# Output projection by token block: whole w_out on chip, merged activations through DRAM

## The chip, the core and the metric

The kernel runs on one NeuronCore of a Trainium2 chip. The metric is device time in microseconds (us) of one execution; lower is better. A profile is one execution recorded by the hardware profiler. The engines are TensorE (PE in the profile, with its weight loads as PEld), VectorE (DVE), ScalarE (ACT), GpSimd (POOL) and SyncE (SP), which here only issues DMA transfers. A "q" behind an engine's name is that engine's instruction queue.

## The reference

One decoder layer over 1,040 tokens (16 meta tokens and 1,024 real ones) with 1,024 channels, in float32:

```python
h = concat(meta, x)
xn = rms_norm(h, g_pre_mix)
# short gated convolution and stick-breaking attention, both on xn
merged = gate_conv * (y_conv @ w_proj_conv) + gate_attn * (o @ w_proj_attn)
mix = merged @ w_out                       # the output projection: the change is here
h = h + rms_norm(mix, g_post_mix)
ffn = conv_gated_mlp(rms_norm(h, g_pre_ffn), w_up_gate, conv_w_ffn, w_down)
h = h + rms_norm(ffn, g_post_ffn)
return h[:, 16:, :]
```

## The kernel before

Only the last 1,026 tokens are needed behind the attention (14 of the meta tokens drop out). They stand as 3 chunks of 342 (CH) or 9 blocks of 114 tokens (QB). Every float32 product is made of three matmuls in fp32r: each operand is split into a rounded part and the rest (`split`, lines 63 to 65: the rounded part by an ACT copy, the rest by a DVE or POOL subtraction), and hi x hi, hi x lo and lo x hi are added up in PSUM. The contraction over 1,024 channels takes 8 steps, so one output tile is 24 matmuls.

The stages around the change, in the order of the program:

- Branch projections, run by `Dense` (lines 80 to 153). An item is one block of 128 output channels, with all 1,026 tokens moving in 3 chunks, 72 matmuls of 342 columns in all. Its weights are loaded two items ahead and split one item ahead (ACT, and POOL for the rest). `item_pc` (8 items) multiplies the convolution branch by its gate and stores it to `m_d` in DRAM. `item_pa` (lines 598 to 613, 8 items) loads the attention gate and that stored product, multiplies by the gate on DVE straight from PSUM (L610), adds on POOL (L611), and splits the merged activations into `mT` (L612), which stands for all tokens on chip in the three slots A, B and C. These slots held `yT`, the convolution output, until the last `item_pc`.
- Output projection (lines 667 to 762). A tile `out_block` has the 114 tokens of a block as its stationary operand and 256 columns of w_out moving (L673 to L675). w_out is split a quarter at a time (`load_wq`, two quarters on chip). The loop takes blocks 0 to 5 through all four quarters, then blocks 6 to 8 through all four, so w_out is loaded and split twice. An evacuation is an ACT Square that sums squares along the row (L679) and a DVE multiplication by g_post into a row buffer of a ring of six (L680).
- Behind the fourth quarter of a block comes `post_block` (lines 682 to 707): the norm's factor from the sum of squares (`rstd_of`, L72 to L77, five small DVE instructions and one ACT square root), h = row x factor + x on DVE in place (L694), the store of h to `h_d` (L695), an ACT Square over h into the x buffer (L697), a second factor, and the normalised row on DVE (L699), which is written over h in the same row buffer. Later `transposed` turns this row by 8 PE transposes (L174) and splits the result (ACT and DVE, L64 and L65 with tile xn) into `xn2`, the FFN's input.
- FFN: `Dense` again, over `xn2`. Its first four chunks are interleaved by hand with the last transposes (lines 765 to 770).

PSUM has 3 buffers for the output projection's tiles, 2 for transposes, 3 for `Dense`. The framework's scheduler fixes the order of instructions on every engine when the kernel is built: among those whose operands it reckons to be ready it takes the first in the order of the program, so a load or a group of matmuls can stand ahead of where the program names it. On the chip each engine then runs its queue strictly in order, and semaphores hold an instruction until its operands are there.

## Time and profile before

| | us |
|---|---|
| median of 3 runs | 2127.32 |
| lowest and highest run | 2126.53, 2127.89 |
| time of the profiled execution | 2128.91 |
| its span, first to last instruction | 2126.8 |

The profiled execution stands 1.6 us above the median; 2.1 us of it lie outside the span. In views of the profile, a gap in square brackets behind a row is how long its engine had been idle ahead of it and what ended that; "granted clock" (PEclk) is the share of TensorE's full clock of 2.4 GHz, 0.50 being its lower level of 1.2 GHz.

### The profile page before, as it was taken

The numbers are of one execution on the slowest core, as the hardware profiler recorded it, in microseconds if no ns is written. First come the engines' busy times: TensorE is split into PE (matmuls) and PEld (weight loads), VectorE is DVE, ScalarE is ACT, GpSimd is POOL, SyncE is SP. The second block draws the span as 40 slices with busy tenths as digits, with TensorE's granted clock in tenths as the row PEclk, the third lists the DMA queues.
The fourth block names the chain that finished last, engine by engine and source line by source line (L and its number), as shares of the span: only waits on it lengthen the run. The fifth ranks groups of instructions, "written<-read, shape, count | busy, mean of one in ns | idle before, by whom it ended". The sixth has DMA issues, their size and how long they took to land.

```text
span 2126.8 us, 31235 instructions
## 1 busy us (share of the span) xinstructions
PE 2048.7 (96%) x12840; PEld 1965.7 (92%) x12840; DVE 1028.5 (48%) x1623; ACT 798.1 (38%) x1667; POOL 706.4 (33%) x597
## 2 busy tenths in 40 slices
PE   5999999999999999999999998899999999999997
PEld 5999999999999999999999998899999999999996
DVE  6455565556555555654231424544333334343436
ACT  4444454545554545544421224432222222222232
POOL 4343444344343534443122432222122221222123
PEclk9999999999999999999999999899999999999999
DMA  3111101111111111111674433411111111111023
GB/s 131 41 50 44 57 31 60 41 50 41 47 44 51 50 41 51 40 60 60 199 228 134 135 126 109 149 63 41 40 54 56 50 40 40 50 60 50 31 80 139
DMA packets 42538, 152.17 MB, mean 72 GB/s; under 512 B 4744, under 2 KB 4744, under 8 KB 42396
## 3 DMA queue, kind: packets, MB, share of 16 engines
q1 hardware_dynamic: 41244, 148.09, 21.2%
q8 instruction: 100, 1.64, 0.3%
q10 hardware_dynamic: 1152, 2.10, 0.3%
q14 instruction: 42, 0.34, 0.1%
HBM read 120.76 MB, written 29.41 MB: 71 GB/s over the span
## 4 chain that ended last, share of the span: by engine, by line
PE 86%; DVE 7%; ACT 3%; DMA 2%; issue 1%; POOL 0%; DVEq 0%; ACTq 0%; SPq 0%; POOLq 0%
PE mm L124 21%; PE mm L125 21%; PE mm L126 20%; PE po L808 3%; PE po L807 3%; PE tp L368 3%; PE po L809 3%; PE av L358 2%; PE av L359 2%; PE z L322 2%; PE z L321 2%; DMA h_d<-owork 1%; DVE fl L332 1%; DVE yy L193 1%; PE po L674 1%
## 5 line engine op out<-in xcount | busy, mean ns | idle before, releaser
L124 PE MATMUL mm<-xnT,whi 128*128 128x342 f32 (+2 forms) x1536 | 508.0, 331 | 3.6 <-ACT xnT L64 3.6
L65 POOL TENSOR_TENSOR wlo<-raw,whi 128x1024 fp32r<-128x1024 f32 x124 | 312.6, 2521 | 576.0 <-ACT whi L64 576.0
L125 PE MATMUL mm<-xnT,whi 128*128 128x342 f32 (+2 forms) x1536 | 495.1, 322 | 0.5 <-DVE xnT L65 0.5
L126 PE MATMUL mm<-xnT,wlo 128*128 128x342 f32 (+2 forms) x1536 | 493.5, 321 | 0.0
L124 PE MATMUL mm<-xn,whi 128*128 128x342 f32 (+1 forms) x1056 | 338.1, 320 | 0.0
L125 PE MATMUL mm<-xn,whi 128*128 128x342 f32 (+1 forms) x1056 | 337.1, 319 | 0.0
L126 PE MATMUL mm<-xn,wlo 128*128 128x342 f32 (+1 forms) x1056 | 336.5, 319 | 0.0
L334 POOL TENSOR_TENSOR be<-be,fl 114x127 f32<-114x127 f32 (+2 forms) x144 | 176.8, 1227 | 404.0 <-DVE fl L332 195.1
L124 PEld LDWEIGHTS mm<-xnT,whi 128*128 128x128 f32 x1536 | 291.1, 190 | 8.4 <-ACT xnT L64 4.2
L125 PEld LDWEIGHTS mm<-xnT,whi 128*128 128x128 f32 x1536 | 291.7, 190 | 2.1 <-DVE xnT L65 1.0
L126 PEld LDWEIGHTS mm<-xnT,wlo 128*128 128x128 f32 x1536 | 290.9, 189 | 0.0
L64 ACT CAST whi<-raw 128x1024 fp32r<-128x1024 f32 x126 | 132.3, 1050 | 265.8 <-PE mm L125 239.8
L332 DVE TENSOR_TENSOR_SCAN fl<-fl 114x128 f32<-114x128 f32 (+2 forms) x144 | 204.9, 1423 | 4.9
L125 PEld LDWEIGHTS mm<-xn,whi 128*128 128x128 f32 x1056 | 199.9, 189 | 2.7
L124 PEld LDWEIGHTS mm<-xn,whi 128*128 128x128 f32 x1056 | 199.2, 189 | 2.8
L126 PEld LDWEIGHTS mm<-xn,wlo 128*128 128x128 f32 x1056 | 199.3, 189 | 0.0
L65 DVE TENSOR_TENSOR al<-tp,ah 128x342 fp32r<-128x342 f32 (+4 forms) x288 | 127.0, 450 | 139.7 <-ACT ah L64 137.3
L814 DVE TENSOR_TENSOR acc<-acc,po 128x512 f32<-128x512 f32 x136 | 93.0, 685 | 189.1 <-PE po L809 189.1
L64 ACT CAST ah<-tp 128x342 fp32r<-128x342 f32 (+4 forms) x288 | 113.1, 398 | 189.7 <-PE tp L368 181.9
L323 ACT ACTIVATE fl<-z 114x348 f32<-114x348 f32 (+10 forms) x240 | 111.5, 465 | 130.7 <-PE z L322 123.4
L368 PE MATMUL tp<-ident,be 114*128 114x114 f32 x720 | 119.5, 263 | 25.6 <-DVE al L65 21.0
L368 PEld LDWEIGHTS tp<-ident,be 114*128 114x128 f32 x720 | 89.1, 138 | 40.2 <-DVE al L65 29.9
(160 smaller groups left out, 3569.6 us busy)
## 6 DMA issues: line engine op xcount, KB each, us to landing
raw<-in_w_in_dram SPq DMA_DIRECT2D x64, 512.0 KB
raw<-in_w_up_gate_dram SPq DMA_DIRECT2D x44, 512.0 KB
raw<-in_w_down_dram SPq DMA_DIRECT2D x22, 512.0 KB
raw<-in_w_out_dram SPq DMA_DIRECT2D x16, 512.0 KB
y_d<-yy SPq DMA_DIRECT2D x8, 513.0 KB
ga_d<-gt SPq DMA_DIRECT2D x8, 513.0 KB
o_d<-ot SPq DMA_DIRECT2D x8, 513.0 KB
gc_d<-gt SPq DMA_DIRECT2D x8, 513.0 KB
```

The lines of the kernel that those rows point to most:

```text
L64: nc.scalar.copy(hi, src)
L65: (lo_engine or nc.vector).tensor_tensor(lo, src, hi.bitcast(F32), op=ALU.subtract)
L124: nc.tensor.matmul(ps, wh, xh, start=(kb == 0), stop=False)
L125: nc.tensor.matmul(ps, wh, xl, start=False, stop=False)
L126: nc.tensor.matmul(ps, wl, xh, start=False, stop=(kb == KB - 1))
L323: nc.scalar.activation(fl[:, c0:c0 + n], z, AF.Sigmoid, scale=-0.125)
L332: nc.vector.tensor_tensor_scan(fl[:, :nk][:, ::-1], fl[:, :nk][:, ::-1], fl[:, :nk][:, ::-1], 1.0, op0=ALU.mult, op1=ALU.min)
L334: nc.gpsimd.tensor_tensor(be[:, 0:nk - 1], be[:, 0:nk - 1], fl[:, 1:nk], op=ALU.mult)
L368: nc.tensor.transpose(tp[:n, QB * j:QB * (j + 1)], blocks[j][0][:, kb * P:kb * P + n], ident[:QB, :QB])
L807: nc.tensor.matmul(ps, th, hi[:, c], start=(j == 0), stop=False)
L808: nc.tensor.matmul(ps, tl, hi[:, c], start=False, stop=False)
L814: nc.vector.tensor_tensor(a, a, ps, op=ALU.add)
```

## The change

`item_pa` no longer builds `mT`. Of its merged activations, blocks 0 and 1 are split at once into two tiles `mb`; the other seven blocks are stored, one DMA for each item, into a new DRAM tensor `mm_d` laid out by token block. w_out is loaded and split once, one block of 128 output columns with each `item_pa`, into slots A, B and C (`w_o`). The output projection then goes block by block, three tiles of 342, 342 and 340 columns each; block b + 1 is loaded from `mm_d` and split (ACT and DVE) while block b is multiplied. The ring of six rows becomes two row buffers, the normalised row is written into the x buffer instead of over h, and transposes follow one block behind. `xn2` has all its slots from the start. The FFN's two first convolution inputs move from the former ring to slot C.

```diff
     m_d = tc.dram_tile([D, NQ], F32, name="m_d")
+    mm_d = tc.dram_tile([7, P, KB * QB], F32, name="mm_d")
...
 
 
     at_ctx.close()
-    slots_r = ctx.enter_context(ExitStack())
-    slotA = ctx.enter_context(pool("slotA", 1, "right"))
-    slots_bc = ctx.enter_context(ExitStack())
-    slotB = slots_bc.enter_context(pool("slotB", 1, "right"))
-    slotC = slots_bc.enter_context(pool("slotC", 1, "right"))
+    slots_abc = ctx.enter_context(ExitStack())
+    slotA = slots_abc.enter_context(pool("slotA", 1, "right"))
+    slotB = slots_abc.enter_context(pool("slotB", 1, "right"))
+    slotC = slots_abc.enter_context(pool("slotC", 1, "right"))
     s_ctx = ctx.enter_context(ExitStack())
     sw = s_ctx.enter_context(pool("sw", 2, "right"))
     gp["p"], gp["n"] = sw, 2
...
     slots_de = ctx.enter_context(ExitStack())
     slotD = slots_de.enter_context(pool("slotD"))
     slotE = slots_de.enter_context(pool("slotE"))
-    slots_f = ctx.enter_context(ExitStack())
-    slotF = slots_f.enter_context(pool("slotF"))
-    wq_ctx = ctx.enter_context(ExitStack())
+    slotF = slots_de.enter_context(pool("slotF"))
+    m_ctx = ctx.enter_context(ExitStack())
+    mpool = m_ctx.enter_context(pool("mblk", 2))
     oT = [slot_tile(pl, "oT") for pl in (slotD, slotE, slotF)]
 
     CH3 = [(0, CH), (CH, CH), (2 * CH, CH)]
...
                 nc.sync.dma_start(m_d[ob * P:(ob + 1) * P, :], g[:, :NQ])
         return (col_block(w_proj_conv, ob), src_of(yT), CH3, evac)
 
-    mT = []
+    mb = {}
+
+    def m_tile(b):
+        mb[b] = mpool.tile([P, 2, KB, QB], F32R, name="mb", tag="mb")
+        return mb[b]
 
     def item_pa(ob):
         st = {}
 
         def evac(ci, a, n, ps):
             if ci == 0:
-                if ob == 0:
-                    mT.extend(slot_tile(pl, "mT") for pl in (slotA, slotB, slotC))
                 st["g"] = sw.tile([P, NT], F32, name="gal", tag="wk")
                 st["m"] = sw.tile([P, NT], F32, name="ml", tag="ld")
                 nc.sync.dma_start(st["g"][:, :NQ], ga_d[ob * P:(ob + 1) * P, :])
...
             g, m = st["g"][:, a:a + n], st["m"][:, a:a + n]
             nc.vector.tensor_tensor(g, g, ps, op=ALU.mult)
             nc.gpsimd.tensor_tensor(g, g, m, op=ALU.add)
-            split(mT[ci][:, 0, ob, :], mT[ci][:, 1, ob, :], g)
+            if ci == 0:
+                for b in range(2):
+                    t = mb.get(b)
+                    if t is None:
+                        t = m_tile(b)
+                    split(t[:, 0, ob, :], t[:, 1, ob, :], g[:, b * QB:(b + 1) * QB])
+            if ci == 2:
+                gv = st["g"][:, 2 * QB:NQ].rearrange("p (b n) -> p b n", n=QB)
+                nc.sync.dma_start(mm_d[:, :, ob * QB:(ob + 1) * QB].rearrange("b p n -> p b n"), gv)
         return (col_block(w_proj_attn, ob), src_of(oT), CH3, evac)
 
     items += [item_pc(ob) for ob in range(8)] + [item_pa(ob) for ob in range(8)]
...
         if k < 8:
             load_split(oT, o_d, k)
             k += 1
-    wq = wq_ctx.enter_context(pool("wq", 2))
-
-    def load_wq(qt):
-        hi = wq.tile([P, KB, 256], F32R, name="wqh", tag="wqh")
-        lo = wq.tile([P, KB, 256], F32R, name="wql", tag="wql")
-        for hf in range(2):
-            raw = wpool.tile([P, D], F32, name="raw", tag="raw")
-            rv = raw.rearrange("p (k n) -> p k n", k=KB)
-            nc.sync.dma_start(raw, w_out[2 * qt + hf])
-            split(hi[:, :, hf * P:(hf + 1) * P], lo[:, :, hf * P:(hf + 1) * P], rv, nc.gpsimd)
-        return hi, lo
-
-    wqs = []
+    w_o = [slot_tile(pl, "w_o") for pl in (slotA, slotB, slotC)]
+    wo_raw = {}
+
+    def load_wo(i):
+        wo_raw[i] = wpool.tile([P, D], F32, name="raw", tag="raw")
+        nc.sync.dma_start(wo_raw[i], w_out[i])
+
+    def split_wo(i):
+        rv = wo_raw.pop(i).rearrange("p (k n) -> p k n", k=KB)
+        for c in range(3):
+            a, e = max(i * P, c * CH), min((i + 1) * P, (c + 1) * CH, D)
+            if a < e:
+                o = slice(a - c * CH, e - c * CH)
+                split(w_o[c][:, 0, :, o], w_o[c][:, 1, :, o], rv[:, :, a - i * P:e - i * P], nc.gpsimd)
+
     for i in range(24):
+        if i % 3 == 0:
+            load_wo(i // 3)
         dense.chunk()
-        if i == 21:
-            wqs.append(load_wq(0))
+        if i % 3 == 1:
+            split_wo(i // 3)
     s_ctx.close()
     psA.close()
 
...
     nc.sync.dma_start(g_post, g_post_mix.partition_broadcast(P))
     nc.sync.dma_start(g_pre2, g_pre_ffn.partition_broadcast(P))
 
-    xn2 = [slot_tile(slotD, "xn2"), slot_tile(slotE, "xn2")]
-    wk = slotF.tile([P, 2, KB, CH], F32, name="owork", tag="t").rearrange("p a k n -> p (a k n)")
-    ring = [wk[:, i * D:(i + 1) * D] for i in range(5)]
-    ring.append(ow.tile([P, D], F32, name="ring5"))
+    xn2 = [slot_tile(pl, "xn2") for pl in (slotD, slotE, slotF)]
 
     ff_items, act, conv_in = [], {}, {}
     dense3 = Dense(ps_mm2, ff_items)
 
-    def out_block(b, qt, hi, lo, ssq):
-        ps = ps_o.tile([P, 512], F32, name="po", tag="po")[:QB, :256]
-        c, o = b // 3, (b % 3) * QB
+    rows = {}
+
+    def load_m(b):
+        if b in mb or b > 8:
+            return
+        raw = mpool.tile([P, KB, QB], F32, name="mraw", tag="mraw")
+        nc.sync.dma_start(raw, mm_d[b - 2].rearrange("p (k n) -> p k n", k=KB))
+        t = m_tile(b)
+        split(t[:, 0], t[:, 1], raw)
+
+    def out_chunk(b, c, ssq):
+        n = min(CH, D - c * CH)
+        ps = ps_o.tile([P, 512], F32, name="po", tag="po")[:QB, :n]
+        m = mb[b]
         for kb in range(KB):
-            mh = mT[c][:, 0, kb, o:o + QB]
-            ml = mT[c][:, 1, kb, o:o + QB]
-            nc.tensor.matmul(ps, mh, hi[:, kb, :], start=(kb == 0), stop=False)
-            nc.tensor.matmul(ps, ml, hi[:, kb, :], start=False, stop=False)
-            nc.tensor.matmul(ps, mh, lo[:, kb, :], start=False, stop=(kb == KB - 1))
-        cs = slice(qt * 256, (qt + 1) * 256)
-        dst = ring[b % 6][:QB, cs]
-        sq = ow.tile([P, 256], F32, name="sq", tag="sq")
-        nc.scalar.activation(sq[:QB], ps, AF.Square, accum_out=ssq[:QB, qt:qt + 1])
-        nc.vector.tensor_tensor(dst, ps, g_post[:QB, cs], op=ALU.mult)
+            mh, ml = m[:, 0, kb, :], m[:, 1, kb, :]
+            wh, wl = w_o[c][:, 0, kb, :n], w_o[c][:, 1, kb, :n]
+            nc.tensor.matmul(ps, mh, wh, start=(kb == 0), stop=False)
+            nc.tensor.matmul(ps, ml, wh, start=False, stop=False)
+            nc.tensor.matmul(ps, mh, wl, start=False, stop=(kb == KB - 1))
+        cs = slice(c * CH, c * CH + n)
+        sq = ow.tile([P, CH], F32, name="sq", tag="sq")
+        nc.scalar.activation(sq[:QB, :n], ps, AF.Square, accum_out=ssq[:QB, c:c + 1])
+        nc.vector.tensor_tensor(rows[b][:QB, cs], ps, g_post[:QB, cs], op=ALU.mult)
 
     def post_block(b, ssq):
         t = b * QB
-        h = ring[b % 6][:QB]
+        h = rows[b][:QB]
         xv = ow.tile([P, D], F32, name="xv", tag="xv", bufs=2)[:QB]
         if b == 0:
             nc.sync.dma_start(xv[0:2], meta_tokens[T0:NMETA, :])
...
         s2 = osml.tile([P, 1], F32, name="s2", tag="s2")
         nc.scalar.activation(xv, h, AF.Square, accum_out=s2[:QB])
         r2 = rstd_of(osml, s2, QB)
-        nc.vector.scalar_tensor_tensor(h, h, r2, g_pre2[:QB], op0=ALU.mult, op1=ALU.mult)
+        nc.vector.scalar_tensor_tensor(xv, h, r2, g_pre2[:QB], op0=ALU.mult, op1=ALU.mult)
 
         def transposed():
             c, o = b // 3, (b % 3) * QB
-            if b == 6:
-                xn2.append(slot_tile(slotA, "xn2"))
-            to_features(xn2[c][:, 0, :, o:o + QB], xn2[c][:, 1, :, o:o + QB], h, QB, ps_tp2)
+            to_features(xn2[c][:, 0, :, o:o + QB], xn2[c][:, 1, :, o:o + QB], xv, QB, ps_tp2)
 
         to_transpose.append(transposed)
 
...
     def item_u(fb):
         def evac(ci, a, n, ps):
             if ci == 0:
-                conv_in[fb] = (wk[:, 3072 + fb * NQ:3072 + (fb + 1) * NQ] if fb < 2 else
+                if fb == 0:
+                    wk = slotC.tile([P, 2, KB, CH], F32, name="owork", tag="t")
+                    ffn["wk"] = wk.rearrange("p a k n -> p (a k n)")
+                conv_in[fb] = (ffn["wk"][:, fb * NQ:(fb + 1) * NQ] if fb < 2 else
                                ffn["u"].tile([P, NQ], F32, name="u", tag="u"))
             u = conv_in[fb]
             nc.scalar.copy(u[:, a:a + n], ps)
...
         ff_items += [item_u(2 * gi), item_u(2 * gi + 1), item_g(2 * gi), item_g(2 * gi + 1)]
 
     to_transpose = []
-    DEFER = 3
-    sums = {}
-    for qi in range(8):
-        qt = qi % 4
-        hi, lo = wqs.pop(0)
-        if qi < 7:
-            wqs.append(load_wq((qi + 1) % 4))
-        blocks = range(6) if qi < 4 else range(6, 9)
-        for b in blocks:
-            if qt == 0:
-                sums[b] = osml.tile([P, 4], F32, name="sums", tag="sums", bufs=9)
-            out_block(b, qt, hi, lo, sums[b])
-            if qi == 6 and b == 6:
-                dense3.load(0)
-            if qi == 7 and b == 6:
-                dense3.prep(0)
-                dense3.load(1)
-            if to_transpose and len(to_transpose) >= (DEFER if qt == 3 else 1):
-                to_transpose.pop(0)()
-            if qt == 3:
-                post_block(b, sums[b])
+    for b in range(9):
+        load_m(b + 1)
+        rows[b] = ow.tile([P, D], F32, name="row", tag="row", bufs=2)
+        sums = osml.tile([P, 3], F32, name="sums", tag="sums")
+        for c in range(3):
+            out_chunk(b, c, sums)
+        if to_transpose:
+            to_transpose.pop(0)()
+        if b == 7:
+            dense3.load(0)
+            dense3.prep(0)
+            dense3.load(1)
+        post_block(b, sums)
 
 
     first = [dense3.run(0), dense3.run(1)]
...
         if to_transpose:
             to_transpose.pop(0)()
     o_ctx.close()
-    wq_ctx.close()
-    slots_f.close()
-    slots_bc.close()
+    slots_abc.close()
+    m_ctx.close()
     fu = ctx.enter_context(pool("fu", 2, "right"))
     fp = ctx.enter_context(pool("ffn", 2))
     fsml = ctx.enter_context(pool("fsml", 4))
```

## Rows read from the trace of the kernel before

**Rows 1.** The page's first part: span, and busy time, share of the span and instructions of each engine.

```profile
span 2126.8 us, 31235 instructions
PE 2048.7 (96%) x12840; PEld 1965.7 (92%) x12840; DVE 1028.5 (48%) x1623; ACT 798.1 (38%) x1667; POOL 706.4 (33%) x597
```

**Rows 2.** Busy time by stretch of the span: start and end in us, length, then busy time (and instructions) of each engine, granted clock, busy share of the 16 DMA engines, and GB/s. The stretches are four items of `item_pa`, the output projection up to the last transposes, and the FFN behind it.

```profile
1165.00:1210.40 45.40, 45.40 (x292) 45.40 (x291) 18.68 (x24) 9.97 (x17) 20.82 (x18) 1.00 0.42 140
...
1242.50:1387.90 145.40, 129.41 (x1010) 127.49 (x1009) 67.11 (x173) 54.03 (x145) 36.47 (x16) 0.94 0.34 114
1388.00:2080.00 692.00, 692.00 (x4003) 655.12 (x4002) 271.51 (x331) 173.46 (x247) 152.03 (x64) 1.00 0.16 52
```

**Rows 3.** TensorE's own instructions in order of time, the first ones of five groups of transposes: start, length, what, and the gap ahead of it. The fifth group stands behind the first chunk of the FFN.

```profile
1311.01 0.84 PE L174 MATMUL tp<-ident,owork 114*128 114x114 f32 x5 [4.12 <-DVE owork L699]
...
1317.01 0.39 PE L174 MATMUL tp<-ident,owork 114*128 114x114 f32 x2 [0.49 <-DVE owork L699]
...
1328.21 0.29 PE L174 MATMUL tp<-ident,owork 114*128 114x114 f32 x1 [4.44 <-DVE owork L699]
...
1343.27 0.43 PE L174 MATMUL tp<-ident,owork 114*128 114x114 f32 x1 [3.67 <-DVE owork L699]
...
1376.02 1.50 PE L174 MATMUL tp<-ident,owork 114*128 114x114 f32 x8 [2.95 <-DVE owork L699]
```

**Rows 4.** Busy time by stretch again (columns as in rows 2), for the four stretches within the output projection in which the granted clock was at its lower level.

```profile
1311.45:1314.86 3.41, 3.41 (x19) 3.41 (x18) 2.07 (x11) 1.78 (x6) 0.00 (x0) 0.50 0.39 156
1328.52:1331.93 3.41, 3.41 (x19) 3.41 (x18) 3.13 (x12) 1.82 (x6) 0.00 (x0) 0.50 0.59 231
1342.17:1348.99 6.82, 5.72 (x28) 5.75 (x29) 4.63 (x10) 2.69 (x7) 0.00 (x0) 0.50 0.56 172
1376.30:1379.71 3.41, 3.41 (x17) 3.41 (x15) 2.52 (x11) 2.37 (x6) 0.00 (x0) 0.50 0.34 139
```

**Rows 5.** The chain of work that ended last, from 1297 to 1388 us: its shares by line, and two of its longest pieces (start, length, what). Below it, from the waits of 1297 to 1388 us: engine, waiting line, what it waited for, us in total, times, longest.

```profile
by line: DMA h_d<-owork 29.0%; DVE owork L694 7.1%; DMA h_d<-ring 6.9%; DVE owork L699 5.7%; PE po L674 5.6%; PE po L675 5.5%; PE po L673 5.5%; PE tp L174 4.8%; issue 4.4%; DVE t L75 4.2%; DVE s L77 2.8%; ACT xv L697 2.2%; ACT sq L679 1.7%;
...
1305.77 9.72 DMA h_d<-owork
1371.22 9.25 DMA h_d<-owork
...
PE tp L174 <- DVE owork L699: 15.7, 5, 4.4
...
DVE owork L699 <- DMA h_d<-owork: 13.9, 7, 3.9
```

**Rows 6.** Two instructions that recur at TensorE's pace: an evacuation's Square (ACT) at the beginning and the end of nine tiles of 256 columns; a load of the stored product (SP's queue) of one item and of the item four later. Then a group of transposes and the matmul behind it (PE).

```profile
1265.45 0.39 ACT L679 ACTIVATE sq<-po 114x256 f32<-114x256 f32 x1 [2.35 <-PE po L675]
...
1290.94 0.38 ACT L679 ACTIVATE sq<-po 114x256 f32<-114x256 f32 x1 [2.36 <-PE po L675]
...
1165.24 0.32 SPq L608 DMA_DIRECT2D ml<-m_d  x1
...
1210.39 0.32 SPq L608 DMA_DIRECT2D ml<-m_d  x1
...
1387.20 0.94 PE L174 MATMUL tp<-ident,owork 114*128 114x114 f32 x8
1387.92 0.40 PE L124 MATMUL mm<-xn,whi 128*128 128x342 f32 x1
```

**Rows 7.** From the end of block 6's last tile to its normalised row, as ACT, DVE and SP's queue ran it (two blocks share some of the small instructions, hence x2).

```profile
1363.72 0.39 ACT L679 ACTIVATE sq<-po 114x256 f32<-114x256 f32 x1 [1.01 <-PE po L675]
...
1366.01 1.29 DVE L694 SCALAR_TENSOR_TENSOR owork<-owork,s,xv 114x1024 f32<-114x1024 f32 x1
...
1367.33 1.06 ACT L697 ACTIVATE xv<-owork 114x1024 f32<-114x1024 f32 x1 [0.29 <-DVE owork L694]
...
1367.33 0.29 SPq L695 DMA_DIRECT2D h_d<-owork  x1
...
1369.60 0.28 DVE L77 TENSOR_TENSOR s<-s,t 114x1 f32<-114x1 f32 x2
...
1374.58 1.29 DVE L699 SCALAR_TENSOR_TENSOR owork<-owork,s,g_pre 114x1024 f32<-114x1024 f32 x1 [3.39 <-DMA h_d<-owork]
```

**Rows 8.** Groups of instructions by line and shape: engine, operation, shape, count | busy us, mean ns of one | idle time ahead of them. The first four are of 1152 to 1242 us (`item_pa`), the last one of 1242 to 1388 us.

```profile
L611 POOL TENSOR_TENSOR gal<-gal,ml 128x342 f32<-128x342 f32 x22 | 20.4, 925 | 38.5 <-DVE gal L610 33.2 <-POOL wlo L65 3.7 <-issue 1.6
L65 POOL TENSOR_TENSOR wlo<-raw,whi 128x1024 fp32r<-128x1024 f32 x7 | 16.9, 2408 | 8.9 <-ACT whi L64 8.9
...
L610 DVE TENSOR_TENSOR gal<-gal,mm 128x342 f32<-128x342 f32 x22 | 11.1, 506 | 14.0 <-PE mm L126 14.0
...
L64 ACT CAST whi<-raw 128x1024 fp32r<-128x1024 f32 x7 | 7.4, 1053 | 18.9 <-PE mm L125 18.4 <-ACT mT L64 0.6
...
L65 DVE TENSOR_TENSOR xn<-tp,xn 128x456 fp32r<-128x456 f32 x16 | 9.8, 628 | 1.4 <-ACT xn L64 1.2
```

**Rows 9.** The DMA queue that all these transfers use (page: packets, MB, share of the time of the 16 DMA engines); and, in `item_pa`, a POOL addition and the load of the attention gate in SP's queue.

```profile
q1 hardware_dynamic: 41244, 148.09, 21.2%
...
1198.15 0.93 POOL L611 TENSOR_TENSOR gal<-gal,ml 128x342 f32<-128x342 f32 x1 [2.85 <-DVE gal L610]
...
1201.89 0.39 SPq L607 DMA_DIRECT2D gal<-ga_d  x1
```

## The prediction

> **What bounds the kernel now.** I began with the busy times of the whole span: TensorE is busy for 2048.7 of 2126.8 us [rows 1], so a change gains only what it takes off TensorE or off TensorE's idle time. The table by stretch says where that lies. In the branch projections TensorE is busy for all of 45.40 us at full clock, and in the FFN for all of 692.00 us; in the output projection it is busy for 129.41 of 145.40 us at a mean clock of 0.94 [rows 2]. So the stretch 1242.5 to 1387.9 us is the one to price.
>
> The gaps on TensorE there stand ahead of transposes: 4.12, 0.49, 4.44, 3.67 and 2.95 us, 15.67 us together, and each was ended by L699, the DVE instruction that makes the normalised row [rows 3]. With each of the four gaps of 2.95 us and more goes a stretch at the lower clock, which begins between 1.1 us ahead of the gap's end and 0.5 us behind it; the gap of 0.49 has none. These stretches last 17.05 us, 15.95 of them busy [rows 4], and half of the busy time, 8.0 us, is what the clock cost.
>
> What L699 waited for: it is written over h, which a DMA is still reading to store it. In the chain of waits that store holds 29.0% of the stretch 1297 to 1388 us, with pieces of 9.72 and 9.25 us, and 13.9 us of DVE's waits are L699 waiting for it [rows 5]. In block 6 everything but that wait took from 1363.72 (Square of the last tile) to 1369.88 (end of L77) and 1.29 for L699, 7.5 us; with the wait L699 ended at 1375.87, 12.2 us [rows 7]. Six blocks reach this tail one tile (2.8 us) apart, so all of it falls due at once.
>
> **The change part by part.**
>
> *The matmuls.* Nine tiles of 24 matmuls with 256 columns took 25.49 us, 2.832 us a tile; four items of three chunks with 342 columns took 45.15 us, 3.762 us a chunk [rows 6]. Before: 36 x 2.832 = 102.0 us. After: 27 x 3.762 = 101.6 us, less 0.2 for the last chunk's 340 columns. Wider tiles therefore gain 0.6 us at most, and I count 0.4. (The 342-column row has 128 stationary columns, the new tiles 114; the 256-column row has 114. I take no gain for that.) The transposes stay, 9 x 0.72 us [rows 6] = 6.5.
>
> *What stalls now cost.* The old stretch holds 102.0 + 6.5 + three FFN chunks of 3.76 = 119.8 us of work in 145.4 us. Lost: 25.6 us, of which the rows above name 15.7 of gaps and 8.0 of clock; the other 1.9 is restarts and smaller gaps.
>
> *The store's wait goes.* The normalised row is written to the x buffer, which nothing stores. Next late: the bare chain of 7.5 us. Per block it has now until the end of the following block, one group of transposes and three chunks: 0.72 + 11.29 = 12.0 us. Other DVE work can get in between: two evacuations of the next block at 0.51, two subtractions of transposes at 0.63 [rows 8], and the subtraction of `load_m` over 912 columns, about 1.2 us by L694's 1.29 for 1024 [rows 7]; together 3.5, so 11.0 of 12.0 us at worst. DVE's whole load of a block is some 8.3 us (three evacuations 1.5, L694 and L699 2.6, subtractions 2.5, small ones 1.7). TensorE waits for nothing here, with 1 us to spare at worst.
>
> *The last block.* Behind block 8 TensorE has only the transposes of block 7 (0.72) and FFN chunks. If the order holds block 8's transposes behind one chunk (3.76), as it held block 6's in the kernel before, they come 4.5 us after the tile, and the chain takes 7.7 (Square and evacuation are wider) to 9.0 us (with block 7's subtractions): a gap of 3.2 to 4.5 us, and 1.7 us of clock. If the order puts a second chunk ahead, 8.2 us are covered and the gap is 0 to 0.8. Bounds 0 and 6.2 us. Before, the wait was in the scheduler's reckoning as well; with a shorter chain it may still go for one chunk. I take 3.0.
>
> *w_out.* Eight loads and splits, not sixteen. In the old projection they ran on POOL and ACT off TensorE's path. Now one goes with each `item_pa`: POOL has 3 x 0.93 + 2.41 + one more 2.41 = 7.6 of 11.29 us [rows 8], ACT 1.05 more. TensorE reads these weights only in the next stage. Nothing on the path; if POOL were full, the cost would be that of the next paragraph.
>
> *The store of merged activations.* Eight DMAs of 7 x 128 pieces of 456 bytes. In SP's queue each waits for POOL's last addition of its item, and behind it stand a w_out load, a weight load two items ahead, and the next items' gate and product loads. The gate's buffer is freed by this DMA's landing and no longer by DVE. Now: that addition ends at 1199.08 and the gate load of the item after next goes out at 1201.89 [rows 9]. After: store out at about 1199.4, landed by at most 9.7 us later (the longest store [rows 5]), so the load goes out at 1209 at worst, 7 us later. Its chunk ends near 1212.3 (items end at 1242.5 minus multiples of 11.29, plus one chunk); the other PSUM buffers cover another 7.5 us. Landing within 7 us hides it. Nothing on the path.
>
> *The reload.* Seven loads, two ahead by the two buffers; the first needs the last store landed: 1242.5 + 2 + 9.7 at worst, then a load of up to 9 us and 2.2 us of splitting, 1265.4, when block 2 is due at 1242.5 + 22.6 + 0.7 = 1265.8. Hidden even then, barely; by h_d's store in block 6 (about 7.2 us) there are 4 us to spare.
>
> *The price of small pieces.* In `item_pa` the 16 DMA engines are busy 0.42 of the time at 140 GB/s [rows 2], 4.74 us an item; w_out adds 0.52 MB, 1.57 us at the same rate. Every packet of this queue takes on average 0.212 x 16 x 2126.8 / 41244 = 175 ns for 3.6 KB [rows 9]. The store is 896 packets: by its bytes (0.41 MB) 1.2 us, by 175 ns a packet 9.8 us. I take it near the bytes: total 7.5 of 11.29 us. The Trainium skill (DMA: Bandwidth & Descriptors, Specifications) says that below 512 bytes a transfer runs under line rate and the DMA engine reads, modifies and writes. If that doubled the 1.2 us, the estimate would be 8.7 of 11.29 us and the time unchanged; no row shows such a store.
>
> *Sum.* After: 101.2 + 6.5 + 11.3 = 119.0 us, 3.0 for the last block, 0.6 for restarts: 122.6 in place of 145.4, 22.8 us less. The profiled execution of 2128.9 would become 2106.1; the median of the runs shown stands 1.6 below it, so I put 2104.5. Without any loss it would be 2127.3 - 26.4 = 2101; less than 2099 would take a matmul rate that no row shows.
>
> **The rivals.**
>
> *A. The block chain takes longer than a block.* If the order on DVE or ACT puts foreign work, or a split waiting for its load, inside the chain, each us beyond 12.0 costs 8 us. The gaps would be short, like the 0.49 that left the clock alone [rows 3, 4]. For it: only 1 us of margin at worst. Against: DVE has 8.3 of 12.0 us. At 13.5 us: 12 us lost, 2116; range 2109 to 2118.
>
> *B. Slower: the branch projections become bound by the DMA engines.* Place: the eight `item_pa`; price: 6.3 + 56 packets per engine x t. It shows from t = 0.11 us (6.2 us of store, with an item's slack spread over eight) and cancels the gain at about 0.16. At 175 ns: 16.1 us an item, 4.8 over TensorE's 11.29, 38 over eight, 28 after some 10 us that loads are issued ahead; gaps that long cost clock too, up to 10 us. 2127 - 23 + 28 + 5 = 2137. For it: its pieces are an eighth of this queue's mean packet, and writes of that size stand in no row. Against: nothing in the trace says that a small packet takes as long as a large one.
>
> *C. It does not do what it says:* transposes still wait, for the reload or the x buffer's load, as long as for the store. TensorE's gaps stay: 2127.
>
> **How the numbers follow.** The forecast, all the gaps gone but part of the last one: 0.69, 2099 to 2109. Rival A 0.16. C and a near cancellation 0.05. B 0.10. The range takes in the forecast and most of A: 2099 to 2115. A difference of 0.2% (4.3 us) is about the least that can be told from no change; so faster 0.86, the same 0.04, slower 0.10.
>
> **What would show it.** Right: the stretch from the first output tile to the last transposes, with three FFN chunks, near 123 us; no gap over 1 us ahead of transposes but the last; clock 1.00 but perhaps once; L699's wait for the store gone; `item_pa` still at 11.29 us an item. Wrong: gaps of equal length in each block (A); TensorE idle before 1242 us with a DMA share near 1 (B); L699 or the transposes waiting for some load (C); block 2 starting late (the reload).

## The result, and the profile after

The changed kernel takes 2109.75 us (median of 4 executions, 2108.01 to 2111.05) against 2127.61 (4 executions, 2126.53 to 2132.42) for the kernel before: ratio 0.9911, 95% interval 0.9894 to 0.9928, some 18 us or 0.9% faster. The profiled execution took 2109.53 us. Of one experiment below (e12_read) the profiled execution was disturbed, at 6384 us against 2105.5 to 2106.0 for its other three, and is left out.

The page's span and busy times of the changed kernel, which answer to [rows 1]:

```profile
span 2107.8 us, 30776 instructions
...
PE 2042.4 (97%) x12624; PEld 1958.1 (93%) x12624; DVE 1008.1 (48%) x1613; ACT 786.6 (37%) x1642; POOL 684.4 (32%) x591
```

TensorE is busy for 6.3 us less and idle for 12.7 us less. Where, the busy times by stretch of the changed kernel say (columns as in [rows 2]): the eight `item_pa`, from there to the first down projection (the output projection and the FFN's first 14 chunks, which are four items and two chunks of a fifth), and the rest of the FFN.

```profile
1151.10:1245.40 94.30, 91.33 (x578) 90.20 (x578) 14.50 (x38) 19.30 (x33) 54.24 (x39) 1.00 0.72 192
1245.40:1407.40 162.00, 161.43 (x1057) 160.72 (x1057) 88.59 (x189) 61.40 (x142) 19.52 (x9) 1.00 0.35 108
1407.40:2095.60 688.20, 688.20 (x3890) 642.80 (x3888) 277.73 (x370) 166.36 (x253) 151.63 (x70) 1.00 0.17 55
```

Cut in the same way, the kernel before has 90.3, 186.9 and 685.5 us. So the output projection gained 24.9 us, and two stages that the prediction left alone lost: the branch items 4.0 us, the FFN 2.7 us. With 1.1 us less ahead of these stages and 0.3 more behind them, that is the 19.0 us between the spans.

In the second stretch the granted clock is 1.00 throughout (0.94 in the output row of [rows 2]; the four stretches of [rows 4] have no successor). Of the gaps ahead of transposes in [rows 3] one is left, of 0.21 us. TensorE's instruction there:

```profile
1361.82 0.39 PE L175 MATMUL tp<-ident,xv 114*128 114x114 f32 x2 [0.21 <-DVE xv L720]
```

The chain of a middle block, as ACT, DVE and SP's queue ran it in the changed kernel, answers to [rows 7]; the last DVE row is the next block's last evacuation:

```profile
1292.86 0.45 ACT L700 ACTIVATE sq<-po 114x340 f32<-114x340 f32 x1 [3.18 <-PE po L697]
...
1293.44 0.51 DVE L701 TENSOR_TENSOR row<-po,g_post 114x340 f32<-114x340 f32 x1 [2.75 <-ACT sq L700]
...
1294.28 1.11 DVE L66 TENSOR_TENSOR mb<-mraw,mb 128x912 fp32r<-128x912 f32 x1
1295.31 1.17 DVE L66 TENSOR_TENSOR xn<-tp,xn 128x456 fp32r<-128x456 f32 x2
...
1297.21 1.28 DVE L715 SCALAR_TENSOR_TENSOR row<-row,s,xv 114x1024 f32<-114x1024 f32 x1
...
1300.98 1.28 DVE L720 SCALAR_TENSOR_TENSOR xv<-row,s,g_pre 114x1024 f32<-114x1024 f32 x1
...
1305.49 0.51 DVE L701 TENSOR_TENSOR row<-po,g_post 114x340 f32<-114x340 f32 x1 [2.80 <-ACT sq L700]
...
1298.53 0.26 SPq L716 DMA_DIRECT2D h_d<-row  x1
```

From the Square of the last tile (L700), where the prediction began to count, to the end of the normalised row (L720, 1302.26) it is 9.4 us, 8.8 of them from the last evacuation (L701), with the reload's split and the other block's subtractions in between; no wait for the store issued at 1298.53. The next block's last evacuation stands 12.05 us behind this one's.

In the branch items the losses are gaps of TensorE of 1.01, 0.15, 0.59 us (ended by the low half of the next item's weight, L66) and 1.22 us (ended by DVE's multiplication by the gate, L612), 2.97 us together; the rest of the 4.0 us is longer busy time (91.33 against 90.30 us). The first of them, and what POOL, ACT and DVE ran up to it:

```profile
1191.12 2.39 POOL L66 TENSOR_TENSOR wlo<-raw,whi 128x1024 fp32r<-128x1024 f32 x1
...
1202.60 2.22 POOL L66 TENSOR_TENSOR w_o<-raw,w_o 128x1024 fp32r<-128x1024 f32 x1 [8.21 <-ACT w_o L65]
1204.78 1.82 POOL L613 TENSOR_TENSOR gal<-gal,ml 128x342 f32<-128x342 f32 x2
1206.55 2.37 POOL L66 TENSOR_TENSOR wlo<-raw,whi 128x1024 fp32r<-128x1024 f32 x1
...
1201.47 1.06 ACT L65 CAST w_o<-raw 128x1024 fp32r<-128x1024 f32 x1 [6.57 <-DMA raw<-in_w_out_dram]
1202.43 1.04 ACT L65 CAST whi<-raw 128x1024 fp32r<-128x1024 f32 x1
...
1204.12 0.51 DVE L612 TENSOR_TENSOR gal<-gal,mm 128x342 f32<-128x342 f32 x1 [7.20 <-DMA gal<-ga_d]
...
1208.98 0.43 PE L127 MATMUL mm<-oT,wlo 128*128 128x342 f32 x1 [1.01 <-POOL wlo L66]
```

POOL runs its queue in order. It stood 8.21 us for w_out's high half, for which ACT stood 6.57 us waiting for the load; behind that stand the split of w_out (2.22 us), two additions (1.82) and only then the weight's low half, which ended when TensorE had waited 1.01 us for it. The gate load was as late as the split: DVE's multiplication, whose product the additions read, stood 7.20 us for it and ended at 1204.63, the split at 1204.82. Either of the two alone would have held the additions here. The next load of w_out waits in SP's queue for the raw buffer that the weight's low half frees, so a late load makes the next one late. The waits of the eight items in the changed kernel (engine, line, what it waited for, us in total, times, longest; the last row is SP's queue):

```profile
POOL w_o L66 <- ACT w_o L65: 33.9, 7, 8.2
ACT w_o L65 <- DMA raw<-in_w_out_dram: 29.2, 7, 6.6
...
DVE gal L612 <- DMA gal<-ga_d: 16.4, 3, 7.2
...
SPq L609 <- DMA mm_d<-gal: 20.6, 6, 5.6
```

In the chain of work that ended last, from 1160 to 1250 us, the gate loads and the stores that they wait for (L609) have the largest shares:

```profile
by line: DMA gal<-ga_d 15.3%; DMA mm_d<-gal 14.1%; PE mm L125 12.4%; PE mm L127 12.1%; PE mm L126 12.1%; POOL gal L613 7.4%; issue 6.8%; DMA raw<-in_w_out_dram 5.2%; POOL wlo L66 4.7%; DVE gal L612 2.8%; PE po L695 1.8%; PE po L696 1.7%; PE
```

### The profile page after: what moved, and what is told of

The parts are those of the page before. It is cut to its first block, busy times and chain, and to the rows that moved or that the text cites. A ratio compares the mean times of both kernels' runs of the same rounds, so it can differ in the third digit from the quotient of the medians.

```text
span 2107.8 us, 30776 instructions
## 1 busy us (share of the span) xinstructions
PE 2042.4 (97%) x12624; PEld 1958.1 (93%) x12624; DVE 1008.1 (48%) x1613; ACT 786.6 (37%) x1642; POOL 684.4 (32%) x591
## 3 DMA queue, kind: packets, MB, share of 16 engines
q10 hardware_dynamic: 1152, 2.10, 0.3%
## 4 chain that ended last, share of the span: by engine, by line
PE 86%; DVE 7%; ACT 3%; DMA 2%; issue 2%; POOL 1%; SPq 0%; DVEq 0%; ACTq 0%; POOLq 0%
PE mm L125 20%; PE mm L126 20%; PE mm L127 20%; PE po L820 3%; PE po L822 3%; PE po L821 3%; PE tp L369 3%; PE av L359 2%; PE av L360 2%; PE z L323 2%; PE z L322 2%; PE po L695 2%; PE po L697 2%; PE po L696 2%; DVE fl L333 1%
## 5 line engine op out<-in xcount | busy, mean ns | idle before, releaser
L66 POOL TENSOR_TENSOR wlo<-raw,whi 128x1024 fp32r<-128x1024 f32 x124 | 312.4, 2520 | 660.9 <-ACT whi L65 660.9
L66 DVE TENSOR_TENSOR al<-tp,ah 128x342 fp32r<-128x342 f32 (+4 forms) x288 | 127.0, 450 | 139.5 <-ACT ah L65 137.5
```

What stands on the lines that cost most here:

```text
L66: (lo_engine or nc.vector).tensor_tensor(lo, src, hi.bitcast(F32), op=ALU.subtract)
```

## The experiments

All are variants of the changed kernel. The last three columns of the table are stages of the profiled execution, in us, cut as above (first matmul of `item_pa`, of the output projection, of the down projection; last matmul of the down projection).

| kernel | time, us | ratio to before, 95% interval | items | output | FFN |
|---|---|---|---|---|---|
| before | 2127.61 | | 90.3 | 186.9 | 685.5 |
| after | 2109.75 | 0.9911 (0.9894 to 0.9928) | 94.3 | 162.1 | 688.1 |
| e4_inplace | 2123.92 | 0.9982 (0.9973 to 0.9992) | 91.5 | 175.3 | 688.1 |
| e1_wraw | 2106.59 | 0.9907 (0.9895 to 0.9919) | 92.6 | 161.5 | 688.1 |
| e3_gate | 2108.97 | 0.9916 (0.9903 to 0.9928) | 96.8 | 161.5 | 688.1 |
| e8_early | 2108.45 | 0.9897 (0.9872 to 0.9922) | 92.1 | 161.5 | 688.1 |
| e2_dve | 2105.76 | 0.9883 (0.9858 to 0.9908) | 90.3 | 161.7 | 688.1 |
| e9_rows | 2105.38 | 0.9885 (0.9856 to 0.9913) | 90.3 | 161.5 | 688.1 |
| e12_read | 2105.51 | 0.9895 (0.9876 to 0.9914) | | | |
| e7_fright | 2105.70 | 0.9903 (0.9890 to 0.9916) | 91.5 | 163.6 | 685.5 |
| e5_pad | 2103.49 | 0.9887 (0.9867 to 0.9906) | 91.4 | 162.1 | 685.3 |
| e11_best | 2104.90 | 0.9881 (0.9856 to 0.9905) | 92.0 | 161.6 | 685.5 |
| e13_dve_place | 2103.31 | 0.9888 (0.9869 to 0.9907) | 90.4 | 161.7 | 685.5 |
| e14_read_dve_place | 2103.99 | 0.9888 (0.9871 to 0.9905) | 90.4 | 161.6 | 685.5 |

The intervals are some 4 us wide to either side, so differences of a few us are read from the stages. The FFN column repeats to some tenths of a us wherever its tiles lie alike. Three other parts vary though their code is the same. The part ahead of the items ended between 1149.0 and 1153.6 us. The output column is 163.6 us in e7_fright, where TensorE waited 1.79 us near the stage's start for an evacuation (0.36 us in after). The items of after, e4_inplace, e7_fright and e5_pad took 94.3, 91.5, 91.5 and 91.4 us: a loss of 1.1 to 4.0 us, of which the profile of after shows the worst. The gap ended by L612, in the last item, stands in all four of them (1.22, 0.91, 0.88 and 0.86 us; its path is the one shown below for e3_gate); the three ended by the weight's low half stand in after alone.

**The wait for the store (e4_inplace).**

```diff
-        nc.vector.scalar_tensor_tensor(xv, h, r2, g_pre2[:QB], op0=ALU.mult, op1=ALU.mult)
+        nc.vector.scalar_tensor_tensor(h, h, r2, g_pre2[:QB], op0=ALU.mult, op1=ALU.mult)
...
-            to_features(xn2[c][:, 0, :, o:o + QB], xn2[c][:, 1, :, o:o + QB], xv, QB, ps_tp2)
+            to_features(xn2[c][:, 0, :, o:o + QB], xn2[c][:, 1, :, o:o + QB], h, QB, ps_tp2)
```

> The changed kernel, with the normalised row written over h again, so that it has to wait for the store of h, and with the transposes reading it there. Both kernels have the same order by token block; this tells the spreading of the blocks from the wait that was taken away. If the wait is what counts: a chain of 7.5 us with 4.7 us of waiting, 12.2 us, and up to 3.5 of other work on DVE inside it, against 12.05 us a block: gaps of 0.2 to 3.7 us ahead of each group of transposes, 2 to 30 us over eight blocks, and some stretches at half clock; middle 2122. If the spreading is what counts: the store (7 to 9 us in the kernel before, where three of them stood together) takes less when it is alone, the chain stays inside the block, TensorE's gaps stay under 1 us together, and the time is 2110 to 2111.

Measured: 2123.92 us (12 executions, 2117.74 to 2127.67; the profiled one is the fastest). Two rows of its waits; two DVE rows, the gap that they lead to, and two more gaps; and its output projection by stretch:

```profile
DVE row L720 <- DMA h_d<-row: 21.1, 9, 3.1
...
PE tp L175 <- DVE row L720: 9.4, 8, 2.4
```

```profile
1336.94 1.29 DVE L715 SCALAR_TENSOR_TENSOR row<-row,s,xv 114x1024 f32<-114x1024 f32 x1 [0.27 <-DVE s L78]
...
1345.46 1.28 DVE L720 SCALAR_TENSOR_TENSOR row<-row,s,g_pre 114x1024 f32<-114x1024 f32 x1 [3.00 <-DMA h_d<-row]
...
1346.89 0.48 PE L175 MATMUL tp<-ident,row 114*128 114x114 f32 x3 [1.89 <-DVE row L720]
...
1371.07 0.39 PE L175 MATMUL tp<-ident,row 114*128 114x114 f32 x2 [2.36 <-DVE row L720]
...
1254.92 0.41 PE L695 MATMUL po<-w_o,mb 128*114 128x342 f32 x1 [2.98 <-DVE row L701]
```

```profile
1240.50:1372.00 131.50, 119.09 (x778) 116.53 (x778) 68.65 (x169) 44.16 (x118) 4.15 (x3) 1.00 0.37 109
```

The store, alone now, holds L720 for 2.3 us a block (21.1 / 9), 3.1 at most, where it had pieces of 9.72 and 9.25 us in the chain [rows 5]. Still eight of the nine groups of transposes wait, 0.5 to 2.4 us each. The wait in the list is less than what the chain loses by it, since other work of DVE falls into it: here L720 begins 7.2 us behind the end of L715 (1338.23), in the changed kernel 2.5 us behind it (1298.49). With 4.7 us more the chain of 8.8 us from the last evacuation becomes 13.5 us, and in the changed kernel the block shown above had its transposes at 1304.7, 11.3 us behind its last evacuation. That gives a gap of some 2 us; 1.89 us was measured in this block.

The profile shows 13.2 us of loss in the stage with the clock at 1.00. The gaps ahead of transposes are 9.4 us of it. The gap of 2.98 us (0.36 us in after) isn't the store's: the first store of h went out at 1259.63. The eleven other executions ran at mean clocks of 0.992 to 0.995 against 0.996 in the profiled one. That suggests that such gaps cost clock in them; their traces weren't kept, so it isn't shown. By the medians all the rest of the change, with its losses in the items and the FFN, gained 4 us of the 18, and the row written to another buffer the other 14. No run writes it to another buffer in the old order of blocks, so what that alone is worth stays open.

**Which of the added parts slows the branch items.** Three theories were named ahead of the first runs: R, the shared ring of raw buffers; G, the gate buffer that only the store's landing frees; S, the store's small pieces.

e1_wraw (R), and below it e3_gate (G):

```diff
-        wo_raw[i] = wpool.tile([P, D], F32, name="raw", tag="raw")
+        wo_raw[i] = sw.tile([P, D], F32, name="wraw", tag="wraw")
```

```diff
-    gp["p"], gp["n"] = sw, 2
+    gp["p"], gp["n"] = sw, 3
...
-                st["g"] = sw.tile([P, NT], F32, name="gcl", tag="wk")
+                st["g"] = sw.tile([P, NT], F32, name="gcl", tag="wk", bufs=3)
...
-                st["g"] = sw.tile([P, NT], F32, name="gal", tag="wk")
+                st["g"] = sw.tile([P, NT], F32, name="gal", tag="wk", bufs=3)
```

> The changed kernel, with w_out's raw rows in two buffers of their own instead of in the ring of two that the weights of the items share. The eight branch items take 94.3 us in the changed kernel and 90.3 in the one before. Theory R (the ring: the load of w_out goes out only when POOL has finished the low half of the next item's weight, lands 8 us later, and POOL's split of it then stands ahead of the next weight split): the items come back to 90.3 to 91.3 us, the gaps of TensorE ended by the weight's low half (L66) go, and the time falls by 3 to 4 us, to about 2106. Theory G (the gate buffer, freed only when the store of the merged activations has landed): the items stay at 94 us, and the waits of the gate loads for that store stay at some 20 us; time 2110. Theory S (the store's 456-byte pieces fill the DMA engines): 94 us as well, 2110.

> The changed kernel, with three buffers instead of two for the gates of the branch items. Theory G: the gate load no longer waits for the last store's landing, the gap of TensorE that DVE's multiplication by the gate ended (1.2 us) goes, and so do the others as far as that wait holds up SP's queue with the weight loads behind it: items at 90.3 to 92 us, time 2106 to 2108. Theory R: that one gap of 1.2 us at most goes, the gaps ended by the weight's low half stay, items 93 to 94 us, time 2109 to 2110. Theory S: 94 us, 2110.

e1_wraw brought the items to 92.6 us, not to 91: the gap moved to the third item. R as the whole cause falls. Its time of 2106.59 us is what R had said, but 1.6 us of the difference lies ahead of the items in its profile. In e3_gate DVE's wait for the gate is gone from the list, and the items took 96.8 us, with the longest gap of all. ACT, DVE and TensorE of e3_gate there:

```profile
1233.08 1.05 ACT L65 CAST w_o<-raw 128x1024 fp32r<-128x1024 f32 x1 [7.47 <-DMA raw<-in_w_out_dram]
1237.28 0.47 ACT L65 CAST mb<-gal 128x114 fp32r<-128x114 f32 x2 [3.15 <-POOL gal L613]
...
1237.60 0.47 DVE L66 TENSOR_TENSOR mb<-gal,mb 128x114 fp32r<-128x114 f32 x2 [14.53 <-ACT mb L65]
...
1238.54 0.65 PE L125 MATMUL mm<-oT,whi 128*128 128x342 f32 x1 [3.74 <-DVE gal L612]
```

G falls: DVE waited 14.53 us for ACT's copy of the blocks 0 and 1, that for POOL's addition, and POOL stood behind its split of w_out, for which ACT had waited 7.47 us. From there two theories were left for the queues: H, the wait for the load at their head, and L, the work itself on POOL. e8_early (with the buffers of e1_wraw), e2_dve and e9_rows, in this order:

```diff
+        if i == 0:
+            load_wo(0)
-        if i % 3 == 0:
-            load_wo(i // 3)
+        if i % 3 == 0 and i < 21:
+            load_wo(i // 3 + 1)
```

```diff
-                split(w_o[c][:, 0, :, o], w_o[c][:, 1, :, o], rv[:, :, a - i * P:e - i * P], nc.gpsimd)
+                split(w_o[c][:, 0, :, o], w_o[c][:, 1, :, o], rv[:, :, a - i * P:e - i * P])
```

```diff
-                nc.sync.dma_start(mm_d[:, :, ob * QB:(ob + 1) * QB].rearrange("b p n -> p b n"), gv)
+                flat = mm_d.rearrange("b p c -> (b p c)").rearrange("(o p n) -> o p n", o=8, p=P)
+                nc.sync.dma_start(flat[ob], st["g"][:, 2 * QB:NQ])
```

> The changed kernel, with w_out's raw rows in two buffers of their own and each row block loaded one item (11.3 us) ahead of its split. The loads took 3.5 to 8 us in the changed kernel, and ACT, which makes the high half, and POOL, which makes the low half, stood waiting for them ahead of the next weight's split. Theory H (that wait at the head of ACT's and POOL's queues is the cause of TensorE's gaps): the wait of ACT for w_out's load goes from 35 us to under 5, no gap is left in the branch items, which take 90.3 to 90.8 us (94.3, 91.5 and 91.5 in the three profiles with the unchanged code), time 2105.5 to 2106.5. Theory L (the added work itself fills ACT or POOL): the load's wait goes, but gaps of 1 us and more ended by the weight's low half stay, items 91.5 to 94 us, time 2107 to 2110.

> The changed kernel, with the low halves of w_out made on DVE instead of POOL. Theory L (POOL's 2.2 us of added work an item is the cause): the items come to 90.3 to 91 us, time 2106. Theory H (the wait for the load at the head of the queues): ACT still waits for the load ahead of the weight's high half, and DVE now waits too, with its multiplications by the gate behind it, so the gaps stay or grow: items 91.5 to 96 us, time 2108 to 2112.

> The changed kernel, with each store of merged activations as 128 whole rows of 3192 bytes in place of 896 pieces of 456 bytes. The bytes are the same, but they land in other places, so the blocks 2 to 8 of the output are computed from the wrong part of the merged activations, at the same time. Theory S (the small pieces cost DMA time that the branch items feel): items 90.3 to 91 us, the loads beside the store land sooner, time 2106. Theory H: the loads' landing changes by a few tenths of a us, items within the 91.5 to 94.3 us of the profiles so far, time 2108 to 2110.

In e8_early the wait for w_out's load shrank only to 16.1 us, because the splits moved ahead with the loads, and the gap stayed. POOL of e8_early, and TensorE behind it:

```profile
1159.81 2.39 POOL L66 TENSOR_TENSOR wlo<-raw,whi 128x1024 fp32r<-128x1024 f32 x1
1162.69 2.20 POOL L66 TENSOR_TENSOR w_o<-wraw,w_o 128x1024 fp32r<-128x1024 f32 x1 [0.49 <-ACT w_o L65]
...
1169.04 2.37 POOL L66 TENSOR_TENSOR w_o<-wraw,w_o 128x352 fp32r<-128x352 f32 x2 [1.01 <-ACT w_o L65]
...
1172.75 2.21 POOL L66 TENSOR_TENSOR w_o<-wraw,w_o 128x1024 fp32r<-128x1024 f32 x1 [0.47 <-ACT w_o L65]
1174.91 2.39 POOL L66 TENSOR_TENSOR wlo<-raw,whi 128x1024 fp32r<-128x1024 f32 x1
...
1177.35 0.42 PE L127 MATMUL mm<-oT,wlo 128*128 128x342 f32 x1 [0.75 <-POOL wlo L66]
```

POOL waited only 0.47 us there and the weight's low half still came too late: with the earlier loads three splits of w_out stand in POOL's queue between one weight's low half and the next, where the changed kernel has one. That is L. And e2_dve, which takes this work off POOL, has no gap left, though ACT still waits 23.5 us for the loads and the gate loads still wait for the store:

```profile
SPq L609 <- DMA mm_d<-gal: 19.9, 6, 5.8
```

Both kernels without loss, e2_dve first, by stretch:

```profile
1149.00:1239.30 90.30, 90.30 (x578) 90.30 (x577) 24.01 (x49) 19.47 (x33) 40.62 (x31) 1.00 0.76 206
```

```profile
1150.50:1240.80 90.30, 90.30 (x578) 90.30 (x577) 15.92 (x40) 19.69 (x33) 55.66 (x40) 1.00 0.62 217
```

e9_rows leaves POOL all its work (55.66 us) and loses nothing either: S as well. The first line is the changed kernel's DMA over 90.3 us, the second that of e9_rows (busy tenths left out):

```profile
DMA packets 9493, 17.19 MB, mean 190 GB/s; under 512 B 5911, under 2 KB 5911, under 8 KB 9489
...
q1 hardware_dynamic: 9489, 17.12, 71.1%
```

```profile
DMA packets 5621, 19.61 MB, mean 217 GB/s; under 512 B 624, under 2 KB 624, under 8 KB 5616
...
q1 hardware_dynamic: 5616, 19.54, 61.5%
```

Per MB the DMA engines took 71.1 / 17.12 = 4.15% against 61.5 / 19.54 = 3.15% of the stretch: a third more with the small pieces. ACT's wait for w_out's loads fell from 29.2 to 15.0 us, POOL's longest wait for ACT from 8.2 to 3.4 us, and no gate load waits for the store. So neither condition made the loss alone: with whole rows POOL has room for the added split, and late loads do no harm when POOL hasn't the split in its queue ahead of the weight. Whole rows let the loads of w_out and of the gate both land earlier; which of the two is the cure, e9_rows doesn't tell.

**The FFN (e7_fright, e5_pad).** TensorE is busy for all of this stage in both kernels, so what changed is the duration of matmuls. The change frees slot A instead of slot F ahead of the FFN, and its pool of activations and down weights starts 21,888 bytes further on each partition. e7_fright, and below it e5_pad:

```diff
+    slotF = ctx.enter_context(pool("slotF", 1, "right"))
     slots_abc = ctx.enter_context(ExitStack())
...
-    slotF = slots_de.enter_context(pool("slotF"))
```

```diff
+    pad = ctx.enter_context(pool("pad")).tile([P, 672], F32, name="pad")
+    nc.gpsimd.memset(pad[:, 0:1], 0.0)
     fp = ctx.enter_context(pool("ffn", 2))
```

> The changed kernel, with its slot F on the other side of on-chip memory, so that the FFN's tiles lie where they lay in the kernel before (in the changed kernel they lie 21,888 bytes further on each partition). The FFN took 2.7 us more in the changed kernel, spread over its steps (6.54 us each instead of 6.49), with TensorE busy for all of it. Theory A (the place of the tiles): steps of 6.49 us, time about 3 us lower, 2107. Theory N (anything else: other transfers, the state of the chip, the merged stage ahead of it): steps stay at 6.54 us, time 2110.

> The changed kernel with 2,688 unused bytes on each partition ahead of the pool that holds the FFN's activations and down weights, so that this pool starts six times 4,096 bytes away from its place in the kernel before, while the pool on the other side stays where the change put it. If the place of this pool counts, and only modulo 4,096 bytes: FFN back at 685.5 us (688.1 in the changed kernel), time about 2107. If the exact place counts, or the other pool's: 688.1 us, time 2105 to 2110 by what the branch items lose. Those are unchanged; a profile shows a loss of 1 to 6 us in them.

The down projection's matmuls in the FFN by line (mean ns of one behind the busy time), of the changed kernel and of e7_fright:

```profile
L820 PE MATMUL po<-dhi,ahi 128*128 128x512 f32 x304 | 120.3, 396 | 0.0
L822 PE MATMUL po<-dlo,ahi 128*128 128x512 f32 x304 | 119.6, 393 | 0.0
L821 PE MATMUL po<-dhi,alo 128*128 128x512 f32 x304 | 118.8, 391 | 0.0
```

```profile
L821 PE MATMUL po<-dhi,alo 128*128 128x512 f32 x304 | 118.9, 391 | 0.0
L820 PE MATMUL po<-dhi,ahi 128*128 128x512 f32 x304 | 118.7, 390 | 0.0
L822 PE MATMUL po<-dlo,ahi 128*128 128x512 f32 x304 | 118.5, 390 | 0.0
```

With the old place all three take 390 to 391 ns and the stage its 685.5 us; e5_pad, which moves that pool (and the small one behind it) still further and leaves the others, has 685.3. So the place of this pool is the cause, and the exact old place isn't needed. Two places don't show which rule of the place it is.

**Together (e11_best, e12_read, e13_dve_place, e14_read_dve_place).** e11_best is e8_early with e3_gate and e7_fright; e13_dve_place is e2_dve with e7_fright; e14_read_dve_place is e13 with e12_read:

```diff
-    mm_d = tc.dram_tile([7, P, KB * QB], F32, name="mm_d")
+    mm_d = tc.dram_tile([D, 7 * QB], F32, name="mm_d")
...
-                gv = st["g"][:, 2 * QB:NQ].rearrange("p (b n) -> p b n", n=QB)
-                nc.sync.dma_start(mm_d[:, :, ob * QB:(ob + 1) * QB].rearrange("b p n -> p b n"), gv)
+                nc.sync.dma_start(mm_d[ob * P:(ob + 1) * P, :], st["g"][:, 2 * QB:NQ])
...
-        nc.sync.dma_start(raw, mm_d[b - 2].rearrange("p (k n) -> p k n", k=KB))
+        nc.sync.dma_start(raw, mm_d[:, (b - 2) * QB:(b - 1) * QB].rearrange("(k p) n -> p k n", p=P))
```

> The changed kernel with w_out's raw rows in their own buffers and loaded an item ahead, three gate buffers, and the FFN's tiles at their old place. If the losses of the branch items are H's (the wait for w_out's load) and the gate's together, and the FFN's 2.7 us are its tiles' place: items 90.3 us, output projection as in the changed kernel, FFN 685.5 us, 2109.75 - 4.0 - 2.7 = 2103. If they stay for the added work: 2105 to 2107.

> The changed kernel with the merged activations stored as whole rows of 3192 bytes and read back by token block in pieces of 456 bytes (1024 to a load), so that the small pieces move from the branch items to the output projection; everything is computed as in the reference. If the small pieces hurt only where transfers are short of time: branch items 90.3 us as with the whole rows before, output projection unchanged (161.5 us to the first down projection), time 2105. If the small loads now hold up the blocks: blocks wait for their load, the output stage grows by some us, time 2107 to 2112.

> The changed kernel with w_out's low halves made on DVE and the FFN's tiles at their old place. Both gains stand in different stages and should add: branch items 90.3 us, output projection as in the changed kernel, FFN 685.5 us, time 2105.8 - 2.7 = 2103. If the items' 90.3 with DVE was luck of one profile: 91 to 92 us there, 2104 to 2105.

> All three together: whole-row stores with the small pieces on the reading side, w_out's low halves on DVE, the FFN's tiles at their old place. If the stores and POOL's work were two conditions of one loss, the second cure brings nothing more: 2103, as with DVE and the place alone, by run time and by stages (90.3, 161.5, 685.5 us). If each held a loss of its own that single profiles missed: 2101 to 2102.

e11_best kept its items' loss (92.0), as L says: its waits for loads are as short as those of e9_rows (15.3 us for w_out, none for the gate), but three splits of w_out stand between two weights as in e8_early. Whether it is that order or the small pieces that sets it apart from e9_rows, no run tells. The time of e12_read, 2105.51 us, is that of e9_rows, but its interval overlaps that of after, and its items weren't seen. e14's output stage of 161.6 us shows that small pieces on the reading side hold up no block. e13 and e14 agree by time and by stage: two cures of one loss. e13_dve_place is the fastest by its median, 2103.31 us (2102.50 to 2107.31); all four executions lie below those of after, while the intervals of the two ratios overlap.

## Why the prediction was right, and where it was not

The forecast of 2104.5 us was 5.2 too low, with the measured time inside the range; against the profiled execution, 2106.1 was said and 2109.5 came.

*The wait that bounds the kernel* was named rightly, and e4_inplace shows it: with the wait put back, 14 of the 18 us go. *The chain of 7.5, at worst 11.0 of 12.0 us* was 9.4 of 12.05. *The clock* came back whole.

*The last block* was mis-sized on the safe side: taken at 3.0 us, it cost 0.21, since the order put two FFN chunks ahead of its transposes, the second case of that step. The stage gained 24.9 us where the sum said 22.8; *the reload* was hidden. The sum has a slip of 0.4 us: 102.0 less the 0.4 counted for wider tiles is 101.6, and it goes on with 101.2.

*"w_out. ... Nothing on the path"* failed, and with it the sign "`item_pa` still at 11.29 us an item" (94.30 / 8 = 11.8). The count of POOL's work was right (7.6 of 11.29 us said, 54.24 us over eight items measured, 6.8 each), but a share says nothing on the order: the step didn't ask what stands behind the split in POOL's and ACT's queues, nor for what the split waits. *"The store ... Nothing on the path"* failed with it. The gate load waited up to 5.6 us for the store, within the 7 us said, but that was not hidden throughout: DVE stood 16.4 us for it in three items, and these stores and loads are 29.4% of the chain that ended last. The wait alone is not the loss: e2_dve has it and loses nothing, and in e3_gate, where DVE's wait is gone, 6.5 us are lost. What wasn't priced at all is that the loads of w_out land later beside the store. *The price of the pieces* itself was near: with 7.5 of 11.29 us said, 0.711 x 11.29 = 8.0 came. In the trace the 456-byte packets took 30.6 ns each on average, 56 x 30.6 = 1.7 us a store, between the 1.2 by bytes and twice that; the 3192-byte rows of e9_rows took 132.5 ns, 8 x 132.5 = 1.1 us for the same bytes. The Trainium skill (DMA: Bandwidth & Descriptors, Specifications) puts transfers below 512 bytes under line rate, and these rows agree.

Rival B had the right place, but not the price: the DMA engines were 71% busy on average, at 1.7 us a store where it needed 6.2, and 1 to 4 us were lost, not 28. Its sign did show in the last item of the changed kernel:

```profile
1230.10:1241.30 11.20, 9.39 (x58) 8.82 (x57) 1.31 (x4) 2.33 (x4) 7.59 (x6) 1.00 0.98 216
```

The share is 0.98 there, and TensorE is idle for 1.8 us. In the last items of e4_inplace, e7_fright and e5_pad, where their one gap of 0.9 us stands, it is 0.95 to 0.99; in e3_gate the gap of 3.74 us stands in an item at 0.69. So full DMA engines go with the loss in the last item, but a loss doesn't need them. Followed back, each gap was ended by work on POOL behind a split of w_out, directly or through ACT's and DVE's work on blocks 0 and 1. A and C did not happen.

*Nothing was said on the FFN.* The change moves its tiles, and the prediction priced the move at nothing without naming it. It cost 2.7 us, about half of the distance between forecast and result.

The two losses are 6.7 us together, and the forecast is less far off than that. The stage gained 2.1 us beyond the sum, and the part ahead of the items took 1.1 us less in the profile of after. The latter is luck: that part varies by 4.6 us between profiles of the same code.

What stays open: why the place of the pool matters, why the same code of the branch items lost 1.1 to 1.2 us in three profiles and 4.0 in one, and what the new order of blocks is worth beside the wait taken away.

## What to carry over

A step that "lies off the path" by its share of busy time needs a second look at its queue: what stands behind it in order, what it waits for, and how late that may come; here 2.2 us of work in a queue used to 58% (54.24 of 94.30 us) put 1 to 4 us on TensorE, and either moving it to another engine or storing whole rows took them off. An in-place write that waits for a store is cheap to take away; in the new order of blocks it was worth 14 of the 18 us. A wait in the list can be shorter than the delay that it makes, where other work of the engine falls into it (3.0 us of waiting, 4.7 us of delay). After a change of on-chip layout, compare the matmul durations of stages that nobody touched.

## What the runs showed of the hardware that was not expected

- With TensorE at full clock and never idle, 128x512 matmuls of the same code took 389 to 392 ns on average, or 391 to 396 ns, by where their operands' pool lay in on-chip memory: moved by 21,888 bytes, the FFN took 688.1 us, in all seven such profiles; at the old place, or 24,576 bytes from it, 685.3 to 685.5, in all six.
- Gaps of 0.5 to 2.4 us, one in nearly every block, left the clock at 1.00 in the profiled execution of e4_inplace, while its twelve executions spread over 10 us and mean clocks of 0.992 to 0.996.
